# Second MLP matrix of the last two token blocks as 2x2 block products with seven products

## The chip, the cores and the metric

One core of one Trainium2 chip runs the whole program. The metric is the time of one execution on the device in microseconds (us). The engines are TensorE (PE; its weight loads, PEld, are shown apart), VectorE (DVE), ScalarE (ACT), GpSimd (POOL) and SyncE (SP), which issues all the DMAs.

## The reference, cut to what matters

The layer takes 2080 tokens of width 1024 (2048 of a prompt and 8 x 4 of samples). Three token mixers come first, then an output projection with a gated residual, and then the MLP, which is what this case is about:

```
h2 = _rmsnorm(x, P['norm2_g'][l]) * (1.0 + sc2) + sh2
ff = jnp.square(jax.nn.relu(h2 @ P['mlp_w1'][l])) @ P['mlp_w2'][l]
x = x + g2 * ff
...
y = _rmsnorm(x, P['final_g'])
```

`mlp_w1` is 1024 x 4096 and `mlp_w2` is 4096 x 1024, all in float32. `g2` has one value per feature for the prompt and one per feature and sample for the samples.

## The kernel before

**Tokens.** The activations lie with features on the 128 partitions and tokens on the columns. The tokens are cut into four blocks: 0, 1 and 3 have 512 columns, block 2 has 544 (512 of the prompt and the 32 of the samples). A first stage projects all four blocks in and runs the mixers, whose work is spread over the program. Then comes, for each block in turn, `out_proj` (L2365), the second norm (`norm2_gen`, L2260) and `mlp` (L2452), while what is left of the mixers runs beside it.

**One product.** TensorE multiplies in a rounded float32 type. Every operand is therefore held as a rounded part (hi) and a remainder (lo), and each product of a 128x128 weight tile with its activations is three matmuls into one PSUM bank: hi*hi, hi*lo and lo*hi. `gemm` (L779) runs 24 of them for one output tile (8 weight tiles deep) where a block is 512 wide. In block 2 it takes the tokens in two pieces of 272 columns, each in a bank of its own (`pieces`, L761), so there 48.

**Weights.** A "half" is 512 columns of weights, that is four 128x128 tiles. Four raw buffers of 1024 columns (`wbuf`, L686) are filled by DMA in the order of use; `wprep` (L708) rounds a half on ACT into a ring of four hi/lo pairs (`NWH`, L684), and `wlow` (L716) makes the remainder. The remainder is split between DVE and POOL in blocks 0 and 1 (288 of 512 columns on POOL); from block 2 on it is all DVE's (`WS.POOL`, L2538). `whalf` (L727) asks for the rounding three halves ahead.

**MLP.** There are 32 tiles of hidden features. `w1_tile` makes one with `gemm`, and `w1_tail` (L2410) turns it into activations: ReLU out of PSUM, square and rounding on ACT, remainder on DVE. Four hidden tiles make a chunk; `w2_chunk` (L2430) multiplies a chunk with the second matrix, one of 8 output tiles at a time (12 matmuls, or 24 in two pieces), and `resid` (L2331) adds the bank, times the gate, into the residual on DVE (`scalar_tensor_tensor` from PSUM; for the samples two small instructions more). So the second matrix takes 768 matmuls of 512 columns in block 3 and 1536 of 272 columns in block 2. Half of the last chunk (`HOLD`, L736) is kept for later: output tiles 4 to 7 of a block run after the next block's `out_proj`, under that block's second norm. `square` (L2387) sums the squares for the final norm, `final_gen` (L2482) applies it and stores y.

**Order.** The instructions are written out by a program that keeps rough clocks of the engines (`Plan`, L113): `pump` (L314) takes the next step of whatever waiting helper is due. On the chip each engine works through its own list in order and waits on semaphores. The seven small state outputs are stored at the very end (L2552 to L2558).

Of the kernel before, what the change touches and what calls it, by code (L numbers as in the profile page):

```python
# [9 lines left out]
F32 = mybir.dt.float32  # L10
# [237 lines left out]
def layer_kernel(ctx: ExitStack, tc: tile.TileContext, d, o, dbg=None):  # L248
# [6 lines left out]
    drp = ctx.enter_context(tc.tile_pool(name="dr", bufs=1, space=DRAM))  # L255
    arena = sbp.tile([128, A_F], F32, name="arena")
    arena_r = sbp.tile([128, A_R], F32R, name="arena_r")
    banks = [psp.tile([128, 512], F32, name=f"bk{i}", tag=f"bk{i}") for i in range(8)]
    GB = Banks(banks[0:3])
    MB = Banks(banks[3:8])  # L260
    M = Mem(arena[:, 0:A_C], A_C)
    M1 = Mem(arena[:, A_C:], A_F - A_C)
    MT = Mem(arena_r[:, 0:26 * W], 26 * W, True)
# [21 lines left out]

    # ------------------------------------------------------------ plumbing
    gens = []
# [26 lines left out]
    def pump(budget=1500, idle=False):  # L314
# [26 lines left out]
        return any_  # L341

    def wait_for(test, what):
        k = 0
        while True:
            r = test()
            if r:
                return r
            if pump(idle=True):
                k = 0  # L350
                continue
# [98 lines left out]

    # ------------------------------------------------------------ constants
    cst = M.get(C_N)
# [28 lines left out]

    lora = M.get(512)
    glu = M.get(512)
    reset = M.get(W)
    V.memset(reset.f, 1.0)
    V.memset(reset.f[:, 0:512:64], 0.0)
    V.memset(reset.f[:, 512:544:4], 0.0)

    halo = M.get(24)
    V.memset(halo.f, 0.0)  # L490
    halo1 = M.get(8)
    V.memset(halo1.f, 0.0)
    sbuf_conv = M.get(192)
    sbuf_shift = M.get(64)
    dt_tm = M.get(17 * 8)
    a_tm = M.get(17 * 8)
    ah_tm = MR.get(17 * 8)
    al_tm = MR.get(17 * 8)
    ssd_S = M.get(512)
    V.memset(ssd_S.f, 0.0)  # L500
    rw_S = M.get(256)
    V.memset(rw_S.f, 0.0)
    eC = M.get(2 * (8 * NB + 8))
    eCv = eC.v("p (f c) -> p f c", f=2)
    s5h = M.get(16)
    s5rot = M.get(2 * 8 * 66)
    s5dec = M.get(512)
# [99 lines left out]

    # ------------------------------------------------------------ adaLN
    mod = M.get(48 * 9)
# [4 lines left out]
    SH1, GA1, SH2, GA2 = 0, 16, 24, 40  # L614
    cs = M.get(8 * 32)
    csv = cs.v("p (k s) -> p k s", k=8)
# [65 lines left out]

    # ------------------------------------------------------------ weights
    NWH = 4  # L684
# [5 lines left out]
    class WS:  # L690
# [3 lines left out]
        pos = 0  # L694
        POOL = 288

    def wload(upto):
        while WS.loaded < min(upto, len(wseq)):
# [3 lines left out]
            WS.loaded += 1  # L702

    def whalves(i):
        hi, lo = wring[i % NWH]
        return hi, lo, wraw[i // 2 % NRB][:, 512 * (i % 2):512 * (i % 2) + 512]

    def wprep(upto):  # L708
        while WS.ready < min(upto, 2 * len(wseq)):
            i = WS.ready  # L710
            wload(i // 2 + 1)
            hi, lo, raw = whalves(i)
            act(hi.r, raw)
            WS.ready += 1

    def wlow(upto):  # L716
        while WS.low < min(upto, WS.ready):
            i = WS.low
            hi, lo, raw = whalves(i)
# [22 lines left out]
    for b in range(NB):  # L742
# [16 lines left out]
        wseq += w2q[7][0:HOLD // 2] if b + 1 < NB else w2q[7]  # L759

# [18 lines left out]
    def gemm(xs, hasS, drop=()):  # L779
        nk = len(xs)  # L780
        got, ws = [], []
        for (c0, c1) in pieces(hasS):
# [4 lines left out]
            for k in range(nk):  # L787
# [7 lines left out]
                for i, (w_, x_) in enumerate(((h_, xh), (h_, xl), (l_, xh))):  # L795
# [8 lines left out]
                    if cnt % SLOT == 0 and cnt < nk * 3:  # L804
                        pump()
            got.append((bk, c0, c1))
        return got

    def gemm2(acts, hasS):
# [4 lines left out]
        for k in range(8):  # L814
            if k > 0 or not WS.pos:
                wait_for(lambda: len(acts) > k, "acts")
            if k == 0:
                pos = WS.pos
                wprep(pos + 2 * nt)
                wlow(pos + 2 * nt)  # L820
                WS.pos += 2 * nt
                wait_for(lambda: len(acts) > k, "acts")
            if k == 6:
# [3 lines left out]
            for u, (m, (c0, c1)) in enumerate(units):  # L827
                hi, lo = (w.r for w in wring[(pos + 2 * m + k // 4) % NWH])
                h_, l_ = hi[:, 128 * (k % 4):128 * (k % 4) + 128], lo[:, 128 * (k % 4):128 * (k % 4) + 128]
# [31 lines left out]

    # ------------------------------------------------------------ token mixers, first stage
    def store(dst, src):
# [311 lines left out]

    # ------------------------------------------------------------ S5
    LWS = -0.30326532985631671
# [373 lines left out]

    # ------------------------------------------------------------ SSD
    def ssd_chunk(b, c):
# [163 lines left out]

    # ------------------------------------------------------------ RWKV, second stage
    def rw_pre(b):
# [374 lines left out]

    # ------------------------------------------------------------ main line
    def mix_flags(b):
# [163 lines left out]
    def norm2_gen(xs, acc, hasS, acts):  # L2260
# [3 lines left out]
        out = []  # L2264
        yield from stats_end(acc[0::2], 1.0 / 1024, 1e-6, hasS, out)
        yield
# [98 lines left out]
    def out_proj(b, acts):  # L2365
# [19 lines left out]
        return xs, new  # L2385

    def square(x, acc, n):  # L2387
        def g():
# [6 lines left out]
            yield  # L2395
            if acc[1] == 7:
# [85 lines left out]
    def final_gen(b, xs, acc):  # L2482
# [4 lines left out]
        yield  # L2487
        yield from stats_end(acc[0::2], 1.0 / 1024, 1e-6, hasS, out)
        yield
# [4 lines left out]
        for k in range(8):  # L2494
            stt(xs[k].f[:, 0:BT], xs[k].f[:, 0:BT], vv(V_GF + k), bk, ALU.mult, ALU.mult)
            if hasS:
                stt(xs[k].f[:, BT:W], xs[k].f[:, BT:W], vv(V_GF + k), b2[:, 0:32], ALU.mult, ALU.mult)
            Q.dma_start(o["y"][k, :, boff[b]:boff[b] + n], xs[k].f[:, 0:n])
            if k % 2:
# [6 lines left out]

    # ------------------------------------------------------------ run
    first4 = [4, 0, 5, 1, 6, 2, 7, 3]
# [28 lines left out]
    for b in range(NB):  # L2537
# [3 lines left out]
        for _ in rest:  # L2541
            pass
        if last is not None:
# [4 lines left out]
        last = (b, xs, hid, acc)  # L2548
    spawn(final_gen(b, xs, acc), 0.4)
    until(("final", NB - 1))  # L2550
    wait_for(lambda: not gens, "end")
    store(o["p_conv"], halo.f)  # L2552
    store(o["p_shift"], halo1.f)
    store(o["s_conv"], sbuf_conv.f)
    store(o["s_shift"], sbuf_shift.f)
    store(o["p_s5"], s5h.f)
    store(o["p_ssd"], ssd_S.f)
    store(o["p_rwkv"], rw_S.f)  # L2558
    if dbg is not None:
        dbg(nc, locals())  # L2560


# [1 line left out]
def _consts():  # L2564
# [163 lines left out]
```

## Time and profile before

| | |
|---|---|
| runs | 2863.2, 2868.24, 2872.96 us, median 2868.24 us |
| profiled execution | span 2863.7 us from its first to its last instruction; no other time of it is given |
| TensorE | 96% busy, granted clock 0.983 of 2.4 GHz in the mean |
| VectorE, ScalarE, GpSimd | 69%, 40%, 23% busy |

The page has one row for all arithmetic (L198), since every instruction goes through one helper; groups are told apart by tile names and shapes. `arena` is the plain float32 memory, `arena_r` the one of rounded operands, `bk` a PSUM bank. A matmul's "busy" is pipelined with its neighbours: its mean duration is longer than the distance between two starts.

### The profile page before, as it was taken

Reading aid. Unit: us, or ns where it says so; the run is one execution under the profiler, and the core shown is the slowest. Engines: PE = TensorE matmul, PEld = TensorE weight load, DVE = VectorE, ACT = ScalarE, POOL = GpSimd, SP = SyncE. Lnnn points to the kernel's source line nnn. Section 1 sums busy time; section 2 is a strip of 40 time slices with the busy share of each in tenths; the row PEclk is TensorE's granted clock in tenths of the full one; section 3 lists DMA queues with packets and bytes.
Section 4 is the critical chain, followed back from the end, with each engine's and each line's share of the span. In section 5 each row is a group of like instructions: output and inputs, shape, how many; then the busy total and the mean of one; then the engine's idle time right before and its main releaser. Section 6 shows DMA issues by size and latency. Waiting matters only on the chain.

```text
span 2863.7 us, 45369 instructions
## 1 busy us (share of the span) xinstructions
PE 2739.5 (96%) x16651; PEld 2265.7 (79%) x16651; DVE 1967.3 (69%) x4567; ACT 1142.5 (40%) x2153; POOL 653.5 (23%) x829
## 2 busy tenths in 40 slices
PE   7999889999999999999999999999999999999997
PEld 4677778877777777777777777778899999888886
DVE  6988996887997877666676778676653535643434
ACT  4354443454335432233443432334534344433342
POOL 1234432233442233322323343321000000000000
PEclk9999999999999999999999999999999999999999
DMA  8467656446553444433434364334222223232222
GB/s 284 155 213 252 201 163 198 164 155 215 170 191 115 144 125 155 146 115 97 159 129 135 118 188 142 120 118 151 96 89 89 89 89 133 82 126 96 99 93 74
DMA packets 302667, 406.26 MB, mean 142 GB/s; under 512 B 85604, under 2 KB 197348, under 8 KB 302444
## 3 DMA queue, kind: packets, MB, share of 16 engines
q1 hardware_dynamic: 302444, 403.36, 42.8%
q8 instruction: 131, 2.15, 0.3%
q14 instruction: 92, 0.75, 0.1%
HBM read 329.67 MB, written 73.62 MB: 141 GB/s over the span
## 4 chain that ended last, share of the span: by engine, by line
PE 62%; DVE 9%; issue 2%; ACT 1%; DMA 1%; POOL 0%; SPq 0%; DVEq 0%; POOLq 0%; ACTq 0%
PE bk L198 62%; DVE arena L198 7%; DVE arena_r L198 2%; ACT arena L198 1%; ACT arena_r L198 1%; DMA arena<-sph 0%; DMA arena<-spk 0%; POOL arena L198 0%; DMA arena<-in_w_out 0%; POOL arena_r L198 0%; DMA arena<-spl 0%; SPq L198 0%; DVEq L198 0%; DVEq L2724 0%; POOLq L198 0%
## 5 line engine op out<-in xcount | busy, mean ns | idle before, releaser
L198 PE MATMUL bk<-arena_r 128*128 128x512 f32 (+1 forms) x11344 | 2284.7, 358 | 61.7 <-DVE arena_r L198 41.5
L198 PEld LDWEIGHTS bk<-arena_r 128*128 128x128 f32 x11344 | 1843.9, 190 | 397.9 <-DVE arena_r L198 65.4
L198 DVE TENSOR_TENSOR arena_r<-arena,arena_r 128x224 fp32r<-128x224 f32 (+2 forms) x981 | 577.7, 610 | 416.9 <-ACT arena_r L198 410.6
L198 ACT ACTIVATE arena_r<-arena 128x512 fp32r<-128x512 f32 (+1 forms) x976 | 581.5, 627 | 468.4 <-PE bk L198 394.3
L198 POOL TENSOR_TENSOR arena_r<-arena,arena_r 128x288 fp32r<-128x288 f32 (+1 forms) x530 | 510.7, 976 | 1055.2 <-ACT arena_r L198 933.2
L198 ACT ACTIVATE arena<-bk 128x512 f32<-128x512 f32 (+8 forms) x619 | 271.9, 459 | 1008.5 <-PE bk L198 798.3
L198 PE MATMUL bk<-arena 128*128 128x128 f32 (+14 forms) x5139 | 540.3, 290 | 50.9 <-DVE arena L198 37.5
L198 PEld LDWEIGHTS bk<-arena 128*128 128x128 f32 (+6 forms) x5139 | 429.7, 152 | 179.7 <-issue 71.2
L198 DVE TENSOR_TENSOR arena<-arena 128x512 f32<-128x512 f32 (+16 forms) x1286 | 515.2, 411 | 51.1 <-ACT arena L198 16.6
L198 DVE SCALAR_TENSOR_TENSOR arena<-bk,arena 128x512 f32<-128x512 f32 (+1 forms) x368 | 235.4, 644 | 269.7 <-PE bk L198 264.0
L198 ACT ACTIVATE arena<-arena 128x512 f32<-128x512 f32 (+4 forms) x445 | 290.1, 664 | 208.1 <-DVE arena L198 189.7
L198 DVE SCALAR_TENSOR_TENSOR arena<-arena 128x512 f32<-128x512 f32 (+9 forms) x605 | 252.2, 430 | 26.6 <-ACT arena L198 6.7
L198 DVE TENSOR_TENSOR arena<-bk,arena 128x512 f32<-128x512 f32 (+4 forms) x277 | 101.2, 381 | 37.0 <-PE bk L198 31.4
L198 POOL TENSOR_TENSOR arena<-arena 128x512 f32<-128x512 f32 (+1 forms) x56 | 73.6, 1320 | 193.5 <-DVE arena L198 100.2
L198 DVE TENSOR_TENSOR arena<-arena,bk 128x512 f32<-128x512 f32 (+2 forms) x163 | 100.4, 627 | 15.3 <-PE bk L198 12.6
L198 DVE SCALAR_TENSOR_TENSOR arena<-arena,bk 64x64 f32<-64x64 f32 (+3 forms) x278 | 91.4, 355 | 27.4 <-PE bk L198 24.1
L198 DVE TENSOR_SCALAR arena<-arena 128x4 f32<-128x4 f32 (+14 forms) x359 | 95.8, 289 | 13.6 <-ACT arena L198 7.8
L198 POOL COPY arena<-arena 128x3 f32<-128x3 f32 (+6 forms) x222 | 70.0, 327 | 47.3 <-ACT arena L198 29.9
L198 ACT ACTIVATE arena<-bk,arena 128x512 f32<-128x512 f32 (+4 forms) x112 | 57.0, 535 | 17.8 <-PE bk L198 16.6
L198 DVE COPY arena<-bk 64x256 f32<-64x256 f32 (+5 forms) x85 | 43.6, 513 | 4.1 <-PE bk L198 2.6
L198 DVE TENSOR_TENSOR_SCAN arena<-arena 128x256 f32<-128x256 f32 (+2 forms) x40 | 36.1, 902 | 1.3
L198 DVE TENSOR_REDUCE arena<-arena 128x4 f32<-128x256 f32 (+1 forms) x34 | 14.0, 412 | 6.7 <-ACT arena L198 6.4
(14 smaller groups left out, 46.3 us busy)
## 6 DMA issues: line engine op xcount, KB each, us to landing
arena<-in_w SPq DMA_DIRECT2D x256, 512.0 KB
arena<-in_w_in SPq DMA_DIRECT2D x88, 512.0 KB
arena<-in_ada_w SPq DMA_DIRECT2D x24, 1024.0 KB
arena<-in_x SPq DMA_DIRECT2D x64, 256.0 KB
arena<-spk SPq DMA_DIRECT2D x32, 512.0 KB
arena<-in_w_out SPq DMA_DIRECT2D x32, 512.0 KB
spk<-arena SPq DMA_DIRECT2D x40, 256.0 KB
spl<-arena SPq DMA_DIRECT2D x33, 256.0 KB
```

Source lines behind the costliest of these rows:

```text
L198: r = fn(*a, **k)
```

## The change

For blocks 2 and 3 the product of the second matrix with a chunk is made in another way. Two neighbouring output tiles, the even and odd hidden tiles of a chunk, and the two halves of the block's tokens (2 x 256 or 2 x 272 columns) form a 2x2 block product, which takes seven products instead of eight, with sums of weight blocks and of activation blocks (S1 to S4 and T1 to T4). A product of one pair of output tiles is two hidden tiles deep: six matmuls of 256 (272) columns. A chunk takes 2 halves x 7 names x 2 pairs = 28 such products. `mlp2` takes the place of `mlp`; `hid_gen` makes the activation sums and their hi and lo parts; `product` writes the matmuls; each product is then added from PSUM by one DVE instruction. The sums of the weights are made by POOL in block 2, stored to device memory, and loaded again in block 3. POOL also makes the remainders of the weight blocks 11, 12 and 22 and of every second half of the first matrix. For this the constant memory of the mixers (4928 columns) is given back after `out_proj(2)` (`tail_setup`, which also stores the states there), and the ring becomes five pairs fed from twelve raw half buffers. The whole last chunk (`rest`) runs after the next block's `out_proj`.

```diff
+    ORDER = ["11", "S2", "12", "S3", "S1", "22", "S4"]
+    CACHED = ["S2", "S3", "S1", "S4"]
...
+            elif name == "S2":
+                self.make("S1")
+                self.sum("S2", t["S1"].f, blk("11"), ALU.subtract)
...
+        def low(self, hi, lo):
+            sm, name = self.sm, self.name
+            (P.tensor_tensor if self.pool else tt)(lo.r, self.src, hi.f, ALU.subtract)
+            sm.drop(name)
...
+    POOLED = ("11", "12", "22")
...
+    def whole(src_, pool=(False, True)):
...
+    def tail_setup():
+        for q in range(NPLAIN, NB):
+            for fl in mix_flags(q) + [("rwb", q)]:
+                until(fl)
+        for dst, t in (("p_conv", halo), ("p_shift", halo1), ("s_conv", sbuf_conv), ("s_shift", sbuf_shift), ("p_s5", s5h), ("p_ssd", ssd_S), ("p_rwkv", rw_S)):
+            store(o[dst], t.f)
...
+    def product(bk, w, col, units, first):
+        for k, (xh, xl, _) in enumerate(units):
+            if 2 * k == len(units):
+                wlow(WS.pos + 2)
...
+            for i, (w_, x_) in enumerate(((w[0], xh), (w[0], xl), (w[1], xh))):
...
+                T.matmul(bk, w_, x_, start=first and k + i == 0, stop=k + 1 == len(units) and i == 2, skip_group_check=True)
...
+        act(bufs[0].r[:, 0:nh], c11)
+        act(bufs[1].r[:, 0:n], e.f[:, 0:n])
+        yield
+        tt(bufs[0].r[:, nh:n], c11, bufs[0].f[:, 0:nh], ALU.subtract)
+        tt(c11, c12, c11, ALU.subtract)
...
+        tt(bufs[2].r[:, 0:n], e.f[:, 0:n], bufs[1].f[:, 0:n], ALU.subtract)
...
+        tt(c12, c22, c12, ALU.subtract)
+        tt(c22, c22, c11, ALU.subtract)
...
+        act(bufs[3].r[:, 0:n], c.f[:, 0:n])
+        tt(c21, c21, c22, ALU.subtract)
...
+            for nm in ORDER:
+                w = whalf()
+                un = H[c][RIGHT[nm]]
+                for e in range(2):
...
+                    key = e, {"12": "11", "22": "S3", "S4": "S1"}.get(nm, nm)
+                    fresh = key not in bks
+                    bk = bks[key] = wide_bank() if fresh else bks[key]
+                    bn = bk[:, 0:nh]
+                    product(bn, w, 256 * e, un, fresh)
+                    if nm == "11" and c == 0:
+                        act(z.f, bn)
+                    elif nm in ("11", "S2"):
+                        tt(z.f, z.f, bn, ALU.add)
+                    elif nm == "12":
+                        add(m0, 0, bn, g0)
+                    elif nm in ("S3", "S1"):
+                        add(m1, 1, bn, g1)
...
+                    if c == 7 and nm == "S2":
+                        add(m1, 0, z.f, g1)
+                        add(m1, 1, z.f, g1)
+                        add(m0, 1, z.f, g0)
...
+                drip(1)
...
+        for c in range(6):
+            w1(4 * c + 4)
+            w1(4 * c + 5)
+            second(c, 0)
+            second(c, 1)
+            w1(4 * c + 6)
+            w1(4 * c + 7)
...
         if last is not None:
-            w2_chunk(*last[0:3], range(HOLD, 8), last[3])
+            if b > NPLAIN:
+                last[2]()
+            else:
+                w2_chunk(*last[0:3], range(HOLD, 8), last[3])
...
-        hid, acc = mlp(b, xs, acts, ys)
+        hid, acc = (mlp2 if b >= NPLAIN else mlp)(b, xs, acts, ys)
...
-    store(o["p_conv"], halo.f)
```

Left out above: six stores like the last line, the other sums, the loads, the choice of banks and, for the samples in block 2, a second accumulator (`Y`) that `close` adds to the residual after the last chunk.

## Rows read from the trace of the kernel before

**Rows 1.** The page: busy time by engine, and the chain that ended last, by engine.

```profile
PE 2739.5 (96%) x16651; PEld 2265.7 (79%) x16651; DVE 1967.3 (69%) x4567; ACT 1142.5 (40%) x2153; POOL 653.5 (23%) x829
...
PE 62%; DVE 9%; issue 2%; ACT 1%; DMA 1%; POOL 0%; SPq 0%; DVEq 0%; POOLq 0%; ACTq 0%
```

**Rows 2.** Windows: stretch, length, busy us of each engine (instructions), granted clock, DMA share, GB/s.

```profile
1500.00:1700.00 200.00, 192.14 (x982) 152.32 (x982) 146.26 (x322) 73.83 (x135) 75.72 (x83) 1.00 0.48 152
...
2060.00:2410.00 350.00, 348.83 (x2783) 348.41 (x2783) 167.58 (x382) 135.09 (x272) 0.00 (x0) 1.00 0.29 100
...
2504.00:2824.00 320.00, 320.00 (x1388) 259.89 (x1387) 136.36 (x216) 120.91 (x205) 0.00 (x0) 1.00 0.29 101
```

**Rows 3.** Timeline of ACT: first evacuation of two neighbouring w1 tiles, in blocks 2 and 3.

```profile
2151.06 0.46 ACT L198 ACTIVATE arena<-bk 128x240 f32<-128x240 f32 x2 [2.60 <-PE bk L198]
...
2157.07 0.46 ACT L198 ACTIVATE arena<-bk 128x240 f32<-128x240 f32 x2 [2.60 <-PE bk L198]
...
2600.43 0.60 ACT L198 ACTIVATE arena<-bk 128x512 f32<-128x512 f32 x1 [2.57 <-PE bk L198]
...
2605.97 0.60 ACT L198 ACTIVATE arena<-bk 128x512 f32<-128x512 f32 x1 [2.57 <-PE bk L198]
```

**Rows 4.** Groups by shape, 2100 to 2300 us (block 2's MLP): busy us, mean ns.

```profile
L198 PEld LDWEIGHTS bk<-arena_r 128*128 128x128 f32 x1597 | 200.2, 188 | 0.0
L198 DVE TENSOR_TENSOR arena_r<-arena,arena_r 128x512 fp32r<-128x512 f32 x66 | 43.9, 686 | 64.7 <-ACT arena_r L198 64.7
L198 ACT ACTIVATE arena_r<-arena 128x512 fp32r<-128x512 f32 x66 | 39.6, 624 | 66.6 <-PE bk L198 66.6
L198 DVE SCALAR_TENSOR_TENSOR arena<-bk,arena 128x272 f32<-128x272 f32 x32 | 16.0, 499 | 2.7
...
L198 DVE TENSOR_TENSOR arena<-arena 128x32 f32<-128x32 f32 x32 | 6.2, 193 | 1.1
```

**Rows 5.** Timeline of DVE: three remainders, one behind the other.

```profile
2602.91 1.90 DVE L198 TENSOR_TENSOR arena_r<-arena,arena_r 128x512 fp32r<-128x512 f32 x3 [3.65 <-ACT arena_r L198]
```

**Rows 6.** Groups by shape, 1500 to 1900 us, where POOL works too: busy us, mean ns.

```profile
L198 PE MATMUL bk<-arena_r 128*128 128x512 f32 x1222 | 304.0, 400 | 8.8 <-DVE arena_r L198 7.6 <-POOL arena_r L198 0.7 <-DVE arena L198 0.3
...
L198 DVE SCALAR_TENSOR_TENSOR arena<-bk,arena 128x512 f32<-128x512 f32 x48 | 35.8, 745 | 27.8 <-PE bk L198 27.6
L198 DVE TENSOR_TENSOR arena_r<-arena,arena_r 128x512 fp32r<-128x512 f32 x28 | 24.6, 880 | 9.2 <-ACT arena_r L198 9.2
...
L198 DVE TENSOR_TENSOR arena<-bk,arena 128x512 f32<-128x512 f32 x26 | 16.9, 682 | 4.5 <-PE bk L198 4.5
...
L198 POOL TENSOR_TENSOR arena<-arena 128x512 f32<-128x512 f32 x10 | 12.4, 1248 | 21.4 <-DVE arena L198 10.7 <-DMA arena<-in_w 7.1 <-PE bk L198 3.6
```

**Rows 7.** Timeline of POOL and DVE at 1600 us.

```profile
1600.56 0.93 POOL L198 TENSOR_TENSOR arena_r<-arena,arena_r 128x288 fp32r<-128x288 f32 x1 [1.95 <-ACT arena_r L198]
1600.74 1.30 DVE L198 TENSOR_TENSOR arena<-arena 128x512 f32<-128x512 f32 x1
...
1602.62 0.68 DVE L198 TENSOR_TENSOR arena<-arena 128x512 f32<-128x512 f32 x1
```

**Rows 8.** Timeline of PE: block 2's out_proj, then from block 3's to its first w1 tiles.

```profile
1979.98 41.67 PE L198 MATMUL bk<-arena_r 128*128 128x272 f32 x312
...
2465.89 1.84 PE L198 MATMUL bk<-arena 128*128 128x1 f32 x16
...
2471.00 6.96 PE L198 MATMUL bk<-arena_r 128*128 128x272 f32 x51
2482.31 12.17 PE L198 MATMUL bk<-arena_r 128*128 128x512 f32 x41 [4.34 <-ACT arena_r L198]
```

**Rows 9.** Timeline of the end.

```profile
2852.93 4.94 SPq L198 DMA_DIRECT2D out_y<-arena  x8
2857.92 0.45 SPq L198 DMA_DIRECT2D out_p_conv<-arena  x1
...
2860.80 0.43 SPq L198 DMA_DIRECT2D out_p_rwkv<-arena  x1
```

More of the change, by code (lines that the diff above doesn't have):

```diff
@@ L1 @@
+import collections
 from contextlib import ExitStack
@@ L341, in pump, with drip @@
         return any_
+    drips = collections.deque()
+    def drip(k=1):
+        while k and drips:
+            g = drips.popleft()
+            try:
+                next(g)
+                drips.appendleft(g)
+            except StopIteration:
+                pass
+            k -= 1
     def wait_for(test, what):
@@ L695, in layer_kernel, with thalf, is_free, tload @@
         POOL = 288
+        flat = 0
+        ops = 0
+        tail = 0
+    tring, traw, tops, tloads, released, early = [], [], [], [], set(), {}
+    def thalf(t, n=1):
+        assert n == 1
+        return traw[t % len(traw)]
+    def is_free(t):
+        if t >= 4 * NRT:
+            return t - 4 * NRT in released
+        return t < 4 * NRT - 8 or WS.low > WS.flat - 4 * NRT + t
+    def tload():
+        while traw and WS.tail < len(tloads):
+            t, n, shape, src_ = tloads[WS.tail]
+            if not all(is_free(q) for q in range(t, t + n)):
+                return
+            for a, b in zip(shape(thalf(t, n)), src_):
+                Q.dma_start(a, b)
+            WS.tail += 1
     def wload(upto):
@@ L708, in wprep @@
     def wprep(upto):
-        while WS.ready < min(upto, 2 * len(wseq)):
+        while WS.ready < min(upto, WS.ops):
             i = WS.ready
+            if i >= WS.flat:
+                tload()
+                op = tops[i - WS.flat]
+                if WS.tail <= op.load:
+                    return
+                op.prep(ring(i)[0])
+                WS.ready += 1
+                for name, load, sm in early.get(i - WS.flat, ()):
+                    if WS.tail > load:
+                        sm.make(name)
+                continue
             wload(i // 2 + 1)
@@ L741, in layer_kernel @@
                 wseq.append((d["w_in"][j], nm))
-    for b in range(NB):
+    for b in range(NPLAIN):
         if b == 0:
@@ new lines, in layer_kernel, with two_ @@
+    for b in range(NPLAIN, NB):
+        made = b == NPLAIN
+        if not made:
+            lead(d["w_out"])
+            for j in range(2, 8):
+                whole(d["w_out"][j], (False, False))
+            group(14, raw2(7, 0))
+            group(15, raw2(7, 2))
+        def two_(c, j):
+            if made:
+                group(2 * c + j // 2, raw2(c, j))
+            else:
+                for x in ORDER:
+                    cached(2 * c + j // 2, x, raw2(c, j))
+        lead(d["w1"])
+        for j in range(2, 4):
+            whole(d["w1"][j])
+        for c in range(7):
+            whole(d["w1"][4 * c + 4])
+            whole(d["w1"][4 * c + 5])
+            if c < 6:
+                two_(c, 0)
+                two_(c, 2)
+            whole(d["w1"][4 * c + 6])
+            whole(d["w1"][4 * c + 7])
+        two_(6, 0)
+        two_(6, 2)
+        if not made:
+            two_(7, 0)
+            two_(7, 2)
@@ L2264, in norm2_gen @@
         out = []
-        yield from stats_end(acc[0::2], 1.0 / 1024, 1e-6, hasS, out)
+        yield from stats_end(acc[0:1] + acc[2:], 1.0 / 1024, 1e-6, hasS, out)
         yield
@@ L2385, in out_proj @@
         return xs, new
+    apart = [7]
     def square(x, acc, n):
@@ L2395, in g @@
             yield
-            if acc[1] == 7:
+            if acc[1] >= apart[0]:
                 acc.append(q)
@@ L2487, in final_gen @@
         yield
-        yield from stats_end(acc[0::2], 1.0 / 1024, 1e-6, hasS, out)
+        yield from stats_end(acc[0:1] + acc[2:], 1.0 / 1024, 1e-6, hasS, out)
         yield
@@ L2505, in final_gen @@
         done.add(("final", b))
+    RIGHT = {"11": "B11", "S2": "T2", "12": "B21", "S3": "T3", "S1": "T1", "22": "T4", "S4": "B22"}
+    AU = [MT]
+    def tail_setup():
[4 more added lines that the diff above has]
+            store(o[dst], t.f)
+        free(lora, glu, reset, s5rot, s5dec, halo, halo1, s5h, ssd_S, rw_S, sbuf_conv, sbuf_shift, dt_tm, a_tm, eC, cs, wdt, mgt_r, ah_tm, al_tm)
+        A1[:] = [M1, M]
+        wait_for(lambda: MS.used == 0, "swap")
+        swap.close()
+        arena_t = ctx.enter_context(tc.tile_pool(name="sb_t", bufs=1, reuse_waits="tile")).tile([128, A_T], F32R, name="arena_t")
+        MT2 = Mem(arena_t, A_T, True)
+        AU.append(MT2)
+        for _ in range(4 * NRT - 8):
+            traw.append(mal(512, [M1]).f)
+        for q in range(8):
+            a = 512 * ((WS.flat + q) % 8)
+            traw.append(wbuf.f[:, a:a + 512])
+        for _ in range(NWT - NWH):
+            tring.append((mal(512, [MR, MT2]), mal(512, [MR, MT2])))
+        tring.extend(wring[(WS.flat + q) % NWH] for q in range(NWH))
+        AT[:] = [MT, MT2]
+        WS.ops = WS.flat + len(tops)
+        tload()
@@ new lines, in side, with wide_bank, get @@
+    def side(U, names, hi, lo, nh):
+        for i, nm in enumerate(names):
+            U[nm].append((hi.r[:, nh * i:nh * i + nh], lo.r[:, nh * i:nh * i + nh], (hi, lo) if i == 0 else ()))
+    def wide_bank():
+        def get():
+            free_ = [(plan.idle(x), i, q, x) for q in (GB, MB) if q is GB or len(MB.free_list) > 2 for i, x in enumerate(q.free_list)]
+            if not free_:
+                return None
+            _, i, q, x = min(free_, key=lambda f: f[0:2])
+            return q.free_list.pop(i)
+        return wait_for(get, "bank")
```

302 lines of the change are left out of this document (271 added, 31 removed).

## The prediction

> **What bounds the kernel now.** I read the page first. TensorE is busy for 96% of the span and the chain that ended last runs over it for 62%; no other engine has a tenth of that chain [rows 1]. So time can come off only where TensorE has fewer columns to stream, or where one of its gaps closes.
>
> Then the stages, by windows. In the MLPs of blocks 2 and 3 TensorE is busy without a break at the full clock (1.00), DVE for 48% and 43%, POOL not at all; DMA is at 0.29 of its engines [rows 2]. There everything beside TensorE has room. In an earlier stretch, with mixers, DVE is at 73% and POOL at 38%, and TensorE still at 96% [rows 2].
>
> Then the pace of TensorE, from the timeline of ACT, which empties one w1 tile after another. Two tiles lie 6.01 us apart in block 2 (48 matmuls of 272 columns) and 5.54 us in block 3 (24 of 512) [rows 3]: 0.1252 and 0.2308 us a matmul. The line through both has a slope of 0.00044 us a column.
>
> **What is removed on TensorE.** Block 2: 1536 matmuls become 8 chunks x 28 products x 6 = 1344 of the same 272 columns. The 192 that go are worth 192 x 0.1252 = 24.0 us. Block 3: 768 x 0.2308 = 177.2 us become 1344 matmuls of 256 columns, a width that the trace lacks. The line gives 0.1252 - 16 x 0.00044 = 0.1182 us. One bound is half a 512-column matmul, 0.1154. The other is 0.1252: in block 2 the weight loads are busy for 200.2 of 200 us [rows 4], so they may be what sets that pace, and then 256 columns are no quicker than 272. I take 0.1182, since 272 is the near row and its slope comes from measured ends: 158.9 us, a gain of 18.4 (22.1 or 9.0 at the bounds). Together **-42.4**.
>
> The Trainium skill (TensorE: Matmul & The Clock Gate, Back-to-back issue gap) gives N/2.4 + 2.5 ns for a warm matmul in isolation, 109 ns at 256 columns; by that, the gain in block 3 would be about 30 us, an estimate. The same formula gives 216 ns at 512 where this trace has 231, so the trace's line stands.
>
> **Stores.** The seven state stores, issued one after another behind y from 2857.92 to 2861.23 us [rows 9], move to `tail_setup`. If the end follows the last issue, that is 3.3 us; if the landing of y sets it, less. I take **-3**. In their new place they stand on SP's queue ahead of the first weights of block 2's MLP (seven issues, some 3.3 us). Their cover is the 48 matmuls x 0.2308 = 11 us of block 1's kept half chunk, and without it TensorE would wait those 3.3 us. The wait for the mixers inside costs nothing: from 1979.98 us on TensorE has only matmuls of block 2's `out_proj` [rows 8].
>
> **What is added, and beside what.** A chunk's 28 products take TensorE 168 x 0.1182 = 19.8 us in block 3 and 21.0 in block 2. In that stretch:
>
> - DVE empties 28 products instead of 8 tiles. A 272-column evacuation lasts 0.50 us and a 512-column remainder 0.69, but three remainders behind one another take 1.90, so each costs 0.61, some 0.08 less than it lasts [rows 4, 5]. For 256 columns I take 0.40, and for a `tensor_tensor` from PSUM 0.34 (0.68 for 512 columns [rows 6], less 256 columns at 1.03 ns, the slope from 193 ns at 32 columns to 686 at 512 [rows 4], and less the overlap). 20 x 0.40 + 8 x 0.34 = 10.7 us.
> - DVE makes 8 weight remainders: 8 x 0.61 = 4.9.
> - DVE makes one pair of hidden tiles ready, five instructions of half the block's columns (0.35) and three of all of them (0.61): 3.6.
>
> DVE's own sum is **19.2 us beside TensorE's 19.8**. In block 2, where more of the evacuations are `tensor_tensor`s, it is 19.0 beside 21.0. The cover is there, and it is thin.
>
> What uses it up is POOL, idle in these stages before. At 1600 us a POOL subtraction runs for 0.93 us; a DVE one, begun 0.18 us later, takes 1.30 us where the next of its kind takes 0.68: it stood for nearly all of the rest of POOL's [rows 7]. Means say the same: with POOL at 38%, DVE's subtraction takes 880 ns against 686, while what reads PSUM keeps its 745 and 682 [rows 2, 4, 6]. So each of the 16 DVE instructions of a stretch that take both operands from SBUF (8 remainders, 8 for the hidden tiles) waits half a POOL instruction whenever POOL holds it off. POOL's 512-column instruction takes 1.25 us [rows 6]; its bounds are 0.93, that of 288 columns [rows 7], and 1.65, the same scaled by columns. In a block 3 stretch POOL has 6 (7.5 us). T = 19.2 + 16 x 0.62 x 7.5/T gives 22.5 us: 2.7 over TensorE's. In block 2 it has the sums of weights too, 12 (15 us): T = 25.0, 4.0 over.
>
> TensorE feels this late. A bank that goes on accumulating ("12" after "11") must be read first, and three products lie between: 3 x 0.71 = 2.1 us of slack in each stretch, after which w1 tiles give DVE 22 us to catch up. So 0.6 and 1.9 us remain of each of the first six chunks of a block: **+15**. Its bounds are 0 (POOL's work falls between DVE's) and 6 x 6.7 = 40 (no slack).
>
> The new waits, and who stands behind them: TensorE's "12", "22" and "S4" wait for DVE; behind them wait all later products. DVE's remainder, held off by POOL, keeps the evacuations behind it. POOL's remainder waits for ACT's rounding, and the sums for two DMAs each.
>
> **The ends**, where no w1 tiles lie between. Block 2's chunk 6 has the loads' remainders for the next `out_proj` in it: some five more, 3 us, on a full DVE: **+4**. Its chunk 7 now lies whole under block 3's second norm. Before, 96 matmuls (12.0 us) lay there in 16.4 us, with a gap of 4.3 [rows 8]. Now 21.0 lie there, which would close the gap; but DVE gains some 8 us of evacuations, 12 additions of `z` (4.3), and 5 for closing and squares, 17 in all, against TensorE's 9: between 0 and 8.6, I take **+5**. At the very end two chunks follow each other: DVE's own 42.0 us (4 halves x 7.8, one hidden pair 3.6, `z` 4.2, squares 3.0) beside 39.7, plus waits, less the slack: **+5** (0 to 8).
>
> **Edits costed at nothing.** ACT has 14 roundings (0.62 each [rows 4]) and one hidden pair (some 4.7) in a stretch, 13.4 of 20 us; without that cover DVE and POOL would start late. DMA: block 2 writes 64 sums of 256 KB, block 3 loads seven quarters for four; at 100 GB/s now, against 152 at 1500 us [rows 2], both fit, and twelve raw halves lie ahead. SP issues about 32 DMAs a chunk, at 0.45 us [rows 9] some 14 of 45 us.
>
> **The sum.** -42.4 - 3 + 15 + 14 = -16.4 us. The profiled span of 2863.7 would become 2847.3. The median of the runs is 4.5 us above that span, the runs spread over 9.8; I take those 4.5 as staying: 2868.2 - 16.4 = **2852 us**. Let X be what DVE gives back (29 here); the time is 2822.8 + X. About 0.3%, 8.6 us, is what a measurement can tell: faster means X under 37, slower X over 54.
>
> **The rivals.**
>
> *All hidden.* X is 0 to 15: time 2823 to 2838, about 2828. For it: DVE's own sum fits, TensorE loses only 8.8 us of 400 to DVE and POOL where both work hard [rows 6]. Against: that stretch has DVE at 73%, here it is at 97% before any wait. 0.25.
>
> *DVE sets the pace, slower.* One mechanism, in the product stretches: each DVE instruction on two SBUF operands stands behind POOL, the slack is used up by the first two, and all of 2.7 and 4.0 us is lost in 8 chunks each, 54 us, with 18 at the ends: X = 72, 2895 us. It decides from X = 54, 3.4 us in each of the 16 stretches. For it: the wait at 1600 us is nearly whole [rows 7], and POOL goes from 0 to over 60% in block 2. Against: the mean extra in [rows 6] is 0.19 us, not the 0.6 of that one case. 0.14. The Trainium skill (SBUF: State Buffer, Who interferes with whom) states the lock as exclusive for the whole instruction; this trace's 1.30 us agrees, and it speaks against giving POOL this work.
>
> *A wash.* X between 37 and 54: 2860 to 2877. Ends or stretches cost half as much again. 0.14.
>
> *256 columns cost what 272 do.* 1344 x 0.007 = 9.4 us less gain: 2861. For it: weight loads without a pause [rows 4]. Against: the pace follows a line with nearly no constant. 0.05.
>
> That the change does not do what it says is left out: the number and width of its matmuls are written out in the loops.
>
> **Numbers.** The forecast (X 15 to 37, 2838 to 2860) has 0.42. Faster: 0.42 + 0.25 = 0.67. Same: 0.14 + 0.05 = 0.19. Slower: 0.14. The range leaves out the slower case alone: 2822 to 2877.
>
> **What would show it.** Right: 2688 matmuls of 256 and 272 columns in the second products, 0.118 us apart in block 3; TensorE's waits in the stretches put down to DVE, 1 to 3 us a chunk; DVE's two-SBUF subtractions above 800 ns there, evacuations unchanged near 0.40 to 0.50; some 29 us of gaps over both MLPs and the stretch between them; the last store 3 us behind y's end gone. Wrong: stretches of 20 us without a gap (all hidden), over 25 in block 3 (DVE paces), a start distance of 0.125 at 256 columns, or waits put down to ACT, POOL's sums or a DMA, which I cost at nothing.

## The result, and the profile after

The median is **2905.2 us** (2901.2 to 2912.3), against 2868.9 us for the kernel before beside it: 1.013 times the time (95% interval 1.011 to 1.015). It is slower, where faster was forecast, and outside the range. The profiled span grew from 2863.7 to 2905.5 us.

The page of the changed kernel, the lines that answer to [rows 1]:

```profile
PE 2734.1 (94%) x17043; PEld 2279.5 (78%) x17043; DVE 2190.5 (75%) x4854; ACT 1206.6 (42%) x2289; POOL 984.8 (34%) x1069
...
PE 51%; DVE 16%; issue 4%; ACT 2%; DMA 2%; POOL 1%; SPq 0%; DVEq 0%; POOLq 0%; ACTq 0%
```

The chain has moved from TensorE to DVE: 11 points less on the one, 7 more on the other. DVE has 223 us more to do, POOL 331. Windows of the two MLPs, in the columns of [rows 2]:

```profile
2100.00:2300.00 200.00, 188.78 (x1450) 185.69 (x1449) 144.61 (x226) 87.56 (x170) 102.83 (x72) 0.98 0.42 131
2560.00:2700.00 140.00, 134.49 (x842) 120.08 (x841) 97.78 (x179) 67.31 (x127) 45.25 (x32) 1.00 0.45 138
```

TensorE, which had no gap here, now stands for 11.2 of 200 us and 5.5 of 140, though DVE is busy for only 72% and 70%. TensorE's waits from 2060 to 2840 us (us in total, times, longest):

```profile
PE bk L204 <- DVE arena L204: 38.8, 23, 5.7
PE bk L204 <- DVE arena_r L204: 3.5, 3, 1.5
PE bk L204 <- ACT arena L204: 2.6, 6, 0.9
PE bk L204 <- ACT arena_r L204: 1.2, 2, 0.7
PE bk L204 <- POOL arena_r L204: 0.4, 1, 0.4
```

42 of 46 us are waits for DVE, and most of them for an evacuation (`arena`; the longest, 5.7 us, is for the statistics of block 2's final norm). Groups by shape, 2100 to 2300 us (busy us, mean ns), to be read beside [rows 4, 6]:

```profile
L204 POOL TENSOR_TENSOR arena_r<-arena,arena_r 128x512 fp32r<-128x512 f32 x40 | 56.6, 1416 | 93.9 <-ACT arena_r L204 86.2 <-PE bk L204 5.2 <-DMA arena<-in_w 2.3
...
L204 DVE TENSOR_TENSOR arena_r<-arena,arena_r 128x512 fp32r<-128x512 f32 x48 | 52.7, 1105 | 19.5 <-ACT arena_r L204 19.5
L204 POOL TENSOR_TENSOR arena<-arena 128x512 f32<-128x512 f32 x32 | 48.0, 1500 | 0.3 <-DMA arena<-in_w 0.3
...
L204 DVE SCALAR_TENSOR_TENSOR arena<-bk,arena 128x272 f32<-128x272 f32 x34 | 15.2, 487 | 0.0
```

DVE's remainder went from 686 to 1105 ns; an evacuation, which reads PSUM, kept its 0.49 us.

**The pace of a chunk.** ACT's timeline, the first w1 evacuation of two chunks one after another in block 2, then the same tile (the second) of two chunks in block 3:

```profile
2165.52 0.40 ACT L204 ACTIVATE arena<-bk 128x272 f32<-128x272 f32 x1 [2.52 <-PE bk L204]
...
2214.72 0.40 ACT L204 ACTIVATE arena<-bk 128x272 f32<-128x272 f32 x1 [2.51 <-PE bk L204]
...
2592.21 0.60 ACT L204 ACTIVATE arena<-bk 128x512 f32<-128x512 f32 x1 [3.94 <-PE bk L204]
...
2637.03 0.60 ACT L204 ACTIVATE arena<-bk 128x512 f32<-128x512 f32 x1 [3.94 <-PE bk L204]
```

49.2 us and 44.8. Block 2's five periods in a row are 50.1, 49.2, 50.3, 50.0 and 49.2 us, 49.8 in the mean; I use 49.7. TensorE's longest wait is about the same in each of them (2.3 us), but in the longer three its clock then falls for a while; two of them as windows, in the columns of [rows 2]:

```profile
2165.52:2214.72 49.20, 46.19 (x362) 45.36 (x361) 35.52 (x56) 21.72 (x43) 25.99 (x18) 1.00 0.42 129
2214.72:2265.06 50.34, 47.61 (x362) 46.87 (x361) 36.30 (x56) 21.84 (x42) 25.62 (x18) 0.97 0.41 126
```

TensorE alone would need 4 x 6.01 + 168 x 0.1252 = 45.1 and 4 x 5.54 + 168 x 0.1182 = 42.0. Before, a chunk took 48.1 and 44.3. So a chunk loses 4.6 us in block 2, more than the 3.0 it gained, and 2.8 in block 3, more than the 2.3 it gained. This period is the measure in all the experiments; a kernel that reaches 45.1 and 42.0 has no gap left in these chunks. The loss it shows is more than the idle time in the windows above, since it also counts waits that hide behind a matmul's long "busy", and half clock.

**Where the time went.** From the two traces, by the same marks (w1 evacuations), less the time of the matmuls between them; spans against spans, so that the left column adds up to the forecast's X = 29:

| stretch | forecast, us | measured, us |
|---|---|---|
| block 2, product stretches 0 to 5 | 11.4 | 6 x 4.6 = 27.6 |
| block 3, product stretches 0 to 5 (1.5 of it a slow fourth w1 tile) | 3.6 | 18.4 |
| last w1 tile of block 2 to third of block 3 | 4 + 5 | 22.2 |
| end, the stores' 3 us taken out | 5 | 10.7 |
| up to block 2's first tiles, and under them | 0 | 4.5 + 3.7 |

The right column adds up to 87, and 2863.7 - 42.4 - 3 + 87 is the new span. Of the last line, 4.5 us lie ahead of block 2's first tile, where `e4` below, the same kernel up to there, has its first evacuation at 2052.2 us and the changed kernel at 2056.9: that part is scatter.

**Inside a stretch.** DVE, POOL and PE from the timeline of one product stretch of block 3, which begins at about 2603.4 us:

```profile
2604.09 0.42 DVE L204 TENSOR_TENSOR arena<-arena,bk 128x256 f32<-128x256 f32 x1 [1.63 <-PE bk L204]
...
2608.35 0.48 DVE L204 SCALAR_TENSOR_TENSOR arena<-bk,arena 128x256 f32<-128x256 f32 x1 [0.22 <-PE bk L204]
2609.07 0.48 DVE L204 SCALAR_TENSOR_TENSOR arena<-bk,arena 128x256 f32<-128x256 f32 x1 [0.23 <-PE bk L204]
2609.47 0.62 DVE L204 TENSOR_TENSOR arena_r<-arena,arena_r 128x256 fp32r<-128x256 f32 x1
...
2617.38 0.69 DVE L204 TENSOR_TENSOR arena_r<-arena,arena_r 128x512 fp32r<-128x512 f32 x1
2617.53 1.70 POOL L204 TENSOR_TENSOR arena_r<-arena,arena_r 128x512 fp32r<-128x512 f32 x1 [5.17 <-ACT arena_r L204]
...
2618.65 1.13 DVE L204 TENSOR_TENSOR arena_r<-arena,arena_r 128x512 fp32r<-128x512 f32 x1
...
2620.40 1.27 POOL L204 TENSOR_TENSOR arena_r<-arena,arena_r 128x512 fp32r<-128x512 f32 x1 [1.18 <-ACT arena_r L204]
2620.49 1.74 DVE L204 TENSOR_TENSOR arena_t<-arena,arena_r 128x512 fp32r<-128x512 f32 x1
2622.15 0.86 DVE L204 SCALAR_TENSOR_TENSOR arena<-bk,arena 128x256 f32<-128x256 f32 x2
2622.77 1.66 PE L204 MATMUL bk<-arena_r 128*128 128x256 f32 x12 [1.49 <-DVE arena L204]
2622.93 0.68 DVE L204 TENSOR_TENSOR arena_r<-arena,arena_r 128x512 fp32r<-128x512 f32 x1
```

Up to 2609 us DVE is on time: it waits for TensorE. Then the hidden tile's instructions begin (2609.47), among evacuations and remainders. A remainder that starts 0.09 us behind POOL's takes 1.74 us where the next takes 0.68; the evacuation behind it is late, and TensorE stands for 1.49 us in front of the 25th of the stretch's 28 products (a "22"). From the stretch's first evacuation to its last, DVE is idle for only 0.9 us, 0.75 of it before 2609:

```profile
2604.09:2626.57 22.48, 20.78 (x166) 20.06 (x165) 21.59 (x45) 12.12 (x22) 8.63 (x6) 1.00 0.48 152
```

In block 2, from 2188.00 to 2212.67 us, DVE is busy for 24.18 of 24.67.

### The profile page after: what moved, and what is told of

Same layout as the page of the kernel before. It is cut to its first block, busy times and chain, and to the rows that moved or that the text cites. A ratio compares the mean times of both kernels' runs of the same rounds, so it can differ in the third digit from the quotient of the medians.

```text
span 2905.5 us, 47928 instructions
## 1 busy us (share of the span) xinstructions
PE 2734.1 (94%) x17043; PEld 2279.5 (78%) x17043; DVE 2190.5 (75%) x4854; ACT 1206.6 (42%) x2289; POOL 984.8 (34%) x1069
## 4 chain that ended last, share of the span: by engine, by line
PE 51%; DVE 16%; issue 4%; ACT 2%; DMA 2%; POOL 1%; SPq 0%; DVEq 0%; POOLq 0%; ACTq 0%
PE bk L204 51%; DVE arena L204 11%; DVE arena_r L204 4%; ACT arena L204 1%; ACT arena_r L204 1%; DMA arena<-in_w 1%; DVE arena_t L204 1%; POOL arena_r L204 0%; POOL arena L204 0%; DMA arena<-sph 0%; SPq L204 0%; DVE arena_b L204 0%; DMA spw<-arena 0%; DMA arena<-in_x 0%; DMA arena<-spk 0%
## 5 line engine op out<-in xcount | busy, mean ns | idle before, releaser
L204 PE MATMUL bk<-arena_r 128*128 128x512 f32 (+2 forms) x10880 | 2208.7, 355 | 82.6 <-DVE arena_r L204 46.8
L204 POOL TENSOR_TENSOR arena_r<-arena,arena_r 128x288 fp32r<-128x288 f32 (+1 forms) x698 | 747.4, 1080 | 1622.3 <-ACT arena_r L204 1454.3
L204 DVE TENSOR_TENSOR arena_r<-arena,arena_r 128x512 fp32r<-128x512 f32 (+2 forms) x927 | 625.0, 687 | 316.5 <-ACT arena_r L204 309.9
L204 ACT ACTIVATE arena_r<-arena 128x512 fp32r<-128x512 f32 (+2 forms) x1099 | 650.2, 622 | 384.2 <-PE bk L204 271.8
L204 DVE TENSOR_TENSOR arena<-arena 128x256 f32<-128x256 f32 (+18 forms) x1112 | 508.2, 463 | 46.2 <-ACT arena L204 16.9
L204 PE MATMUL bk<-arena 128*128 128x128 f32 (+12 forms) x3957 | 404.4, 271 | 56.0 <-DVE arena L204 44.1
L204 DVE SCALAR_TENSOR_TENSOR arena<-bk,arena 128x512 f32<-128x512 f32 (+3 forms) x400 | 225.9, 586 | 144.4 <-PE bk L204 143.4
L204 DVE SCALAR_TENSOR_TENSOR arena<-arena 128x512 f32<-128x512 f32 (+12 forms) x623 | 267.6, 443 | 30.2 <-ACT arena L204 9.7
L204 DVE TENSOR_TENSOR arena<-arena,bk 128x272 f32<-128x272 f32 (+4 forms) x363 | 176.4, 505 | 46.4 <-PE bk L204 42.5
L204 PE MATMUL bk<-arena_t,arena_r 128*128 128x272 f32 (+1 forms) x848 | 159.3, 293 | 19.5 <-DVE arena L204 16.3
L204 PEld LDWEIGHTS bk<-arena_t,arena_r 128*128 128x128 f32 x848 | 127.2, 193 | 24.2 <-issue 17.4
```

What stands on the lines that cost most here:

```text
L204: r = fn(*a, **k)
```

## The experiments

**1 to 4: which work is too much.** The theory, from the forecast's own sum: DVE's work in a stretch, with the waits for POOL, lasts longer than TensorE's products (T), and all of the difference is lost. The rivals: DVE's own work is too much, POOL or not; or a bank that goes on accumulating has a fixed turn-around. That POOL's remainders come late is ruled out by TensorE's 0.4 us of waits for POOL.

`e1` leaves out POOL's remainders (11, 12, 22), so the third matmul of those products takes the rounded part instead; POOL keeps the sums of block 2.

```diff
-            (P.tensor_tensor if self.pool else tt)(lo.r, thalf(self.t), hi.f, ALU.subtract)
+            if not self.skip:
+                (P.tensor_tensor if self.pool else tt)(lo.r, thalf(self.t), hi.f, ALU.subtract)
...
+                if nm not in CACHED:
+                    w = (w[0], w[0])
```

> Left out: POOL's remainders of the weight blocks 11, 12 and 22 (the third matmul of each of those products takes the rounded part again), so that POOL has no work in block 3's product stretches and only the sums in block 2's. The period of a chunk is 49.8 us in block 2 and 45.0 in block 3 of the changed kernel; by TensorE's matmuls alone it would be 45.1 and 42.0. Theory (DVE held off by POOL): block 3 42.0 to 42.5, block 2 about 46.4, in all some 40 us less, 2865 +- 10. Rival 1 (DVE's own work is too much, POOL or not): both periods as they are, 2905 +- 6. Rival 2 (the turn-around of a bank that goes on accumulating, whatever DVE's load): as they are, 2905 +- 6.

Measured: 2874.9 us, 1.003 times the time before (1.001 to 1.005); chunks of 48.0 us, where 46.4 was expected, and 43.0. POOL isn't idle in block 3, as the expectation has it: it still makes the remainders of the first matrix's second halves, 18.7 of the 140 us from 2560 on (45.3 in the changed kernel), two of them in each product stretch. DVE's remainder falls from 870 to 758 ns there, and 1.0 of the 2.8 us stays. So the remainders left out are worth 30 us, and POOL's share of the loss is at least that.

`e2` cuts POOL's instructions in two of 256 columns: the same work, held for half as long at a time.

```diff
-            P.tensor_tensor(t.f, a, b, op)
+            for q in (0, 256):
+                P.tensor_tensor(t.f[:, q:q + 256], a[:, q:q + 256], b[:, q:q + 256], op)
```

> Every POOL instruction of the last two MLPs (sums and remainders) is cut into two of 256 columns; the work is the same, the longest time for which POOL can hold DVE off is halved. Theory (DVE held off by POOL): waits halve, block 3 about 43.4 a chunk, block 2 about 46.9, 2872 +- 12. Rival 1 (DVE's own work) and rival 2 (turn-around): 45.0 and 49.8 stay, 2905 to 2910.

Measured: 2883.8 us, 1.004 (1.002 to 1.006); chunks of 48.3 and 44.0. The groups of [rows 4]'s window in this kernel:

```profile
L204 POOL TENSOR_TENSOR arena_r<-arena,arena_r 128x256 fp32r<-128x256 f32 x85 | 75.8, 913 | 72.3 <-ACT arena_r L204 68.6 <-PE bk L204 3.7
L204 POOL TENSOR_TENSOR arena<-arena 128x256 f32<-128x256 f32 x66 | 57.0, 884 | 0.0
...
L204 DVE TENSOR_TENSOR arena_r<-arena,arena_r 128x512 fp32r<-128x512 f32 x52 | 48.4, 936 | 18.8 <-ACT arena_r L204 18.8
```

POOL is busier than before (133 against 105 us), and yet DVE's remainder is 169 ns shorter and the kernel 21 us faster. It is how long POOL holds at a time that DVE pays for. It gave 12 us less than the middle of what was expected; two halves together last longer than one whole (1.83 us beside 1.42 for remainders, 1.77 beside 1.50 for sums), which is likely why.

`e3` leaves out DVE's four remainders (S1 to S4), so those products too take the rounded part twice; POOL does all it did.

```diff
+            if not self.skip:
...
+                if nm in CACHED:
+                    w = (w[0], w[0])
```

> Left out: DVE's remainders of the weight sums S1 to S4, 8 of a chunk's instructions (the third matmul of those products takes the rounded part again); POOL's work stays. Theory (DVE held off by POOL) and rival 1 (DVE's own work): DVE's sum falls to 14.3 us in a stretch of 19.8, waits included under 17, so TensorE sets the pace: 42.0 and 45.1 a chunk, 2845 +- 12. Rival 2 (turn-around of a bank, whatever DVE's load): an evacuation comes as late as before, 49.8 and 45.0 nearly stay, over 2890.

Measured: 2855.7 us, 0.995 (0.993 to 0.997); chunks of 46.2 and 42.4. With 8 of its instructions gone DVE nearly keeps up, POOL's hold or not (1.1 and 0.4 us of a chunk stay): 49.5 us come back.

`e4` gives all of block 3's remainders to POOL, to see whether DVE's count or POOL's hold weighs more.

```diff
-    POOLED = ("11", "12", "22")
+    POOLED = ("11", "S2", "12", "S3", "S1", "22", "S4")
```

> In block 3 all fourteen remainders of a chunk's weight blocks go to POOL instead of six; DVE keeps evacuations and hidden tiles. Theory (DVE held off by POOL in instructions on two operands of SBUF): DVE's own sum falls to 14.3 us, it has 8 such instructions left that POOL (17.5 of 19.8 us busy) can hold off, together 18.6: TensorE sets the pace or nearly, 42.0 to 43.0 a chunk, 2885 to 2892. Rival 1 (DVE's own work alone): 42.0, the same. Rival 3 (any work on POOL slows the stretch): longer than 45.0, above 2910. Block 2 keeps 49.8 under all of them.

Measured: 2899.5 us, 1.010 (1.007 to 1.013); chunks of 49.7 and 43.8, where 42 to 43 was expected. POOL's group, 2560 to 2700 us, and one stretch, first evacuation to last:

```profile
L204 POOL TENSOR_TENSOR arena_r<-arena,arena_r 128x512 fp32r<-128x512 f32 x60 | 84.6, 1433 | 57.4 <-ACT arena_r L204 50.5 <-PE bk L204 7.0
...
2642.58:2663.71 21.13, 20.48 (x165) 19.69 (x165) 19.22 (x38) 12.12 (x22) 18.27 (x13) 1.00 0.47 142
```

POOL goes from 32% to 59% and takes back part of what DVE is spared: the remainders left on DVE last 1183 ns instead of 870. The time from the last w1 tile to the end grew from 67.0 to 71.1 us. A miss in size, and a telling one: DVE's 19.2 us in the stretch are near the 18.6 expected and less than TensorE's 19.8, and yet 1.8 us of a chunk are lost. The sum of DVE's work fits; it doesn't come at the right time.

**5 and 6: when, not how much.** If the work fits by its sum but not in the stretch, moving the hidden tile's instructions out of it should be enough, with nothing removed. `e5` steps them only under the w1 tiles (and, with no w1 tiles left, in chunk 6). Were DVE too busy in all, nothing would change.

```diff
-                drip(1)
+                if c == 6:
+                    drip(1)
```

> One edit to the changed kernel: the steps that make a pair of hidden tiles ready are no longer written between the products of chunks 0 to 5 but only between the w1 tiles. The work is the same. Theory (DVE is late in the product stretches, by its own work and by POOL's hold): DVE's own sum in a stretch falls by 3.6 us, from 19.2 to 15.6 beside 19.8 of TensorE's, with waits 17.7: 42.2 a chunk in block 3 (44.8 in the changed kernel), about 45.3 in block 2 (49.7), in all some 42 us less, 2863 +- 12. Rival 2 (turn-around of a bank): nothing moves, over 2898. Rival 4 (hidden tiles then come too late for the next chunk): periods longer than in the changed kernel.

Measured: 2868.9 us, 1.000 (0.998 to 1.001), 36 us less; chunks of 45.7 and 42.2 us. Its windows, the last one a stretch of block 3 from first evacuation to last:

```profile
2100.00:2300.00 200.00, 198.59 (x1578) 197.71 (x1578) 147.74 (x249) 97.66 (x186) 115.22 (x79) 1.00 0.43 138
2560.00:2700.00 140.00, 140.00 (x852) 124.53 (x851) 99.56 (x180) 70.84 (x130) 46.57 (x34) 1.00 0.42 132
...
2618.58:2638.22 19.64, 19.64 (x165) 19.55 (x165) 17.56 (x37) 10.38 (x19) 8.41 (x6) 1.00 0.54 183
```

DVE and POOL are as busy as in the changed kernel, a little more in fact, and TensorE has no gap in block 3. DVE's remainder still takes 867 ns there; in the stretch DVE is now busy for 17.6 of 19.6 us. So it is neither the sum of the work nor the hold alone, but both on top of 3.6 us of other work in the same 20 us.

`e6` is `e5` and `e2` together.

> The edit of e5 and POOL's instructions cut in halves as in e2. Theory: in the stretches TensorE already sets the pace, so the second edit adds little there and shortens what stands under the norm and at the end: 5 to 10 us under e5. If the hold by POOL still costs in the stretches after e5, it is more, up to 20.

Measured: 2858.7 us, 0.997 (0.996 to 0.998); chunks of 45.1 and 42.2. Block 2 reaches TensorE's own pace, and the kernel is below the one before. What is still lost lies at the ends.

**7 and 8: one that missed, and the turn-around.** `e7` makes block 2's final norm due 15 us later in the planner, since its statistics stand in the way between the blocks: TensorE waits 5.74 us for them.

```diff
-            spawn(final_gen(last[0], last[1], last[3]), 0.4)
+            spawn(final_gen(last[0], last[1], last[3]), 0.4, plan.clk["PE"] + 15000 if b > NPLAIN else 0.0)
```

> One edit to the changed kernel: block 2's final norm is put off by 15 us of the plan's clock. In the changed kernel TensorE stands for 5.7 us behind its statistics, in front of the third w1 tile of block 3, and then runs at half clock: from the first to the third w1 tile 17.7 us instead of 5.5. Theory (an instruction written too early blocks TensorE's list): that falls to about 7, in all 8 to 11 us less, 2896 +- 5. Rival (DVE simply has that much to do there): the gap moves to another place, 2903 to 2907.

Measured: 2904.6 us, 1.013 (1.010 to 1.016). The wait is the same, 5.75 us: the planner's clock is rough, and the step came out in the same place. It says nothing on the theory.

`e8` tests the turn-around: two more products (one name, both pairs) between a bank's "11" and its "12", and so also between "S3" and "22"; between "S1" and "S4" three stay.

```diff
-    ORDER = ["11", "S2", "12", "S3", "S1", "22", "S4"]
+    ORDER = ["11", "S2", "S3", "12", "S1", "22", "S4"]
```

> One edit to the changed kernel: product 12 comes after S3 instead of before it, so that five products instead of three lie between the two uses of its bank; the work is the same. Rival 2 (turn-around of an accumulating bank): the wait in front of 12 goes, at least 1 us a stretch, 2890 or less. Theory (DVE's pace): no change, 2900 to 2912, periods 49.7 and 44.8.

Measured: 2903.8 us, 1.013 (1.010 to 1.016); chunks of 49.1 and 45.0. More distance in the order gives 0.6 us in block 2 and costs 0.2 in block 3: a fixed turn-around in front of "12" and "22" isn't what paces these stretches.

**9 and 10: the ends.** `e9` is `e6` with block 2's final norm 40 us later, enough to move it.

```diff
+            spawn(final_gen(last[0], last[1], last[3]), 0.4, plan.clk["PE"] + 40000 if b > NPLAIN else 0.0)
```

> On top of e6 (hidden tiles made ready between w1 tiles, POOL in halves): block 2's final norm is put off by 40 us of the plan's clock; e7's 15 us left its statistics in the same place of TensorE's list, so e7 told nothing. Theory (an instruction written too early blocks TensorE's list): the wait of 3.6 us behind the statistics and the half clock after it go, first to third w1 tile of block 3 15.2 to 7 us, in all 6 to 9 us less than e6, 2851 +- 4. Rival (DVE has that much to do there whatever the order): the gap moves, 2857 to 2860.

Measured: 2851.5 us, 0.993 (0.991 to 0.996). TensorE's timeline in the changed kernel, then in this one:

```profile
2521.62 1.46 PE L204 MATMUL bk<-arena_r 128*128 128x512 f32 x4 [0.49 <-ACT arena_r L204]
2528.83 4.14 PE L204 MATMUL bk<-arena 128*128 128x1 f32 x20 [5.74 <-DVE arena L204]
2532.83 7.36 PE L204 MATMUL bk<-arena_r 128*128 128x512 f32 x20
```

```profile
2518.02 0.53 PE L204 MATMUL bk<-arena_t,arena_r 128*128 128x256 f32 x3
2518.38 2.33 PE L204 MATMUL bk<-arena 128*128 128x1 f32 x20
2520.57 0.60 PE L204 MATMUL bk<-arena_r 128*128 128x256 f32 x3
```

The same 20 one-column matmuls, ahead of ready work in the one and between products in the other: the wait (5.74 us, and 3.57 in `e6`) is gone. Against `e6`, the time from block 2's last w1 tile to block 3's third falls by 8.8 us (138.3 to 129.6), but block 3's first chunk, where the norm's matmuls now stand, takes 47.4 us instead of 42.2. So the rival is half right: in the two profiled executions 5.2 us come back and 3.6 stay gained; the rest of the 7 us between the medians isn't placed.

`e10` is `e9` with the first half of block 2's last chunk ahead of block 3's `out_proj` again, as the kernel before had it.

```diff
+        second(7, 0)
...
-            second(7, 0)
```

> On top of e9: the first half of block 2's last chunk is made before block 3's out_proj, as in the kernel before, and only the second half is kept for the stretch under block 3's second norm. Theory (under the norm DVE has more to do than TensorE, so products kept for that place cost more than they fill): 3 to 8 us less than e9. Rival (TensorE needs the products there as cover): a gap opens before block 3's first w1 tile, 3 to 10 us more than e9.

Measured: 2845.4 us (2837.4 to 2856.0), 0.992 (0.989 to 0.995); span 2835.4. The sign and size are as expected, but its runs spread over 19 us and its interval overlaps that of `e9`: that it beats `e9` isn't settled. That both beat the kernel before is.

## Why the prediction was wrong

- **TensorE's gain: right.** Starts lie 119 ns apart at 256 columns and 126 at 272 (medians), forecast 118 and 125. The 42.4 us are there: `e9` reaches 45.1 and 42.2 us a chunk. "256 columns cost what 272 do" is refuted.
- **The stores: right.** The last event follows y's last issue by some 3 us, as it followed the last store's before.
- **DVE's instructions and POOL's hold: right.** An evacuation of 256 columns lasts 0.474 us, two of them 0.86 (0.40 each was taken, 0.43 measured). DVE's two-SBUF subtractions passed 800 ns: 870 in block 3, 1105 in block 2. T was forecast at 22.5 and 25.0 us; DVE is busy for 21.6 and 24.2 in the two stretches read above.
- **The 2.1 us of slack: wrong, and this is the step that failed.** The forecast let three products' distance in the order absorb 2.1 us of each stretch, and booked 1.9 and 0.6 us of loss. With T as measured, 1.8 and 3.2 us over TensorE's time, the same slack would have left nothing in block 3 and 1.1 us in block 2. Measured were 2.8 and 4.6: all of T's excess and a little more. The bound given for "no slack", 40 us, was right within 6, and the forecast chose 15. The slack would have to be there when DVE falls behind; but DVE idles early in a stretch and has its hidden tile, remainders and POOL's hold together later (the timeline above). `e4` shows that the sum doesn't decide: 1.8 us are lost with DVE's 19.2 us below TensorE's 19.8. `e5` gets the loss back by moving 3.6 us, with nothing removed, and in `e8` more distance for two of the three banks bought 0.6 us in block 2 and nothing in block 3.
- **The ends: twice too small.** 22 us for the 9 around block 3's norm, 11 for the 5 at the end. Not forecast at all was that the final norm's statistics would stand at the head of TensorE's queue there (5.74 us); moving them in `e9` gained 3.6 us there, by the profiled executions. How much of the rest is half clock behind the gaps and how much DVE isn't settled.
- **The rivals.** "DVE sets the pace, slower" (2895 us, 0.14) was the right mechanism, its stretch loss 54 over 16 stretches against some 46 measured over 12, and its ends 18 against some 41 (22 + 11 + 8). That its time is within 10 us is thus partly luck: one term is too large and the other too small. Its evidence, the nearly whole wait at 1600 us [rows 7], outweighed the mean of [rows 6] that was held against it: a mean over 28 instructions of which 19 lasted 0.67 to 0.69 us, nearly all without POOL running at their start, and nine 1.28 to 1.30. "All hidden" fell with TensorE's first gap. The chance of 0.67 for faster rested on the slack; with the bound of no slack taken as likely as the rest, it couldn't have been above a half.

The Trainium skill (SBUF: State Buffer, Who interferes with whom) calls the port that DVE and GpSimd share an exclusive lock; this trace agrees: 1.74 us beside 0.68.

## What to carry to other kernels

When TensorE's work is cut, compare the helpers with the new, shorter stretch in which their results are due, and not with the stage: at 70% busy DVE still made TensorE wait, and moving 3.6 us of its work by half a chunk was worth 36 us. Slack that is counted in the order of instructions may cover nothing of what arrives in one lump; unless a row shows it used, the bound without it belongs in the forecast at full weight. And a POOL instruction can hold off a DVE one with both operands in SBUF for nearly as long as it lasts, so cut it short.

## What the runs showed of the hardware that was not expected

**The hold is the rest of POOL's instruction, and can be computed.** Two cases stand in the stretch above. DVE's remainder at 2618.65 has 0.58 us of POOL's left and takes 0.45 longer than 0.68; the one at 2620.49 has 1.18 left and takes 1.06 longer. Each time it is the rest, less 0.13 us; so it is for all 33 of DVE's 512-column instructions on two SBUF operands that start under a POOL instruction, with no other behind it, between 2540 and 2840 us. Evacuations there take 0.476 us under POOL and 0.472 without. POOL is held in the same way: its 1.70 us at 2617.53, where one that meets no DVE at its start takes 1.30, begin with 0.54 us of DVE's left. So halving POOL's instructions helps although POOL is busy 27% longer (`e2`).

**A gap can cost TensorE twice, and so can one-column matmuls.** Windows of the changed kernel: the whole time between the blocks, then behind the statistics' wait, and after it; then one of `e9`, and one of the kernel before:

```profile
2520.00:2560.00 40.00, 33.77 (x147) 27.37 (x146) 27.29 (x55) 17.02 (x34) 8.44 (x6) 0.83 0.32 101
2529.00:2533.00 4.00, 4.00 (x21) 3.94 (x22) 0.38 (x2) 0.00 (x0) 0.00 (x0) 0.50 0.45 131
2533.00:2538.00 5.00, 5.00 (x12) 3.94 (x13) 4.48 (x18) 0.00 (x0) 0.00 (x0) 0.50 0.02 3
2541.00:2559.00 18.00, 18.00 (x82) 14.72 (x82) 14.75 (x27) 8.80 (x18) 5.42 (x4) 1.00 0.42 137
...
2522.00:2524.00 2.00, 2.00 (x11) 2.00 (x11) 1.30 (x9) 0.63 (x1) 0.00 (x0) 0.50 0.00 0
...
2497.00:2500.00 3.00, 3.00 (x10) 2.37 (x10) 2.76 (x13) 2.89 (x5) 0.00 (x0) 0.65 0.00 0
```

The granted clock is at 0.50, which is 1.2 GHz, behind a wait of 5.74 us, and back at 2.4 GHz by 2541. In block 2 the same follows a wait of 2.34 us that ends at 2247.70: the window from 2248 to 2252 us has 0.57. The five chunks have this wait alike, 2.29 to 2.34 us long. The clock over the next 4 us is 0.58, 1.00, 0.57, 0.66 and 1.00, and the periods are 50.1, 49.2, 50.3, 50.0 and 49.2 us. No wait is needed: in `e9` and in the kernel before, TensorE has work at hand, and the clock falls right behind 20 one-column matmuls (2518.38 to 2520.71 and 2494.31 to 2496.64). Behind the same 20 in `e10`, at 2503.82, it stays at 1.00: such a dip doesn't come every time. The forecast priced gaps at their own length, and in block 2 this is part of the "little more" above.
